# A written order for three engines in the expert stage of a transformer block

## The chip, the cores and the metric

The kernel runs on one core of a Trainium2 chip. Five engines work side by side, each through its own list of instructions, in order: TensorE (PE, matmuls), VectorE (DVE), ScalarE (ACT), GpSimd (POOL) and SyncE (SP, which issues transfers); the DMA engines move the data. The metric is the time of one execution on the device in microseconds; the lower the better.

## The reference, cut to what matters

One block over 512 tokens of width 1024: a mixer of two kinds of attention, then a sparse expert layer. Only the expert layer is touched.

```python
logits = (hf @ router_w + router_b).astype(jnp.float32)
top_val, top_idx = lax.top_k(logits, TOP_K)          # 4 of 32 experts per token
gate = jax.nn.softmax(top_val, axis=-1)
...
def expert_block(args):                              # up to 128 tokens of one expert
    e, toks, wts = args
    u = hf[toks] @ w1[e] + b1[e]                     # 1024 -> 2048
    g_, lin = u[:, :D_FF], u[:, D_FF:]
    g_ = jnp.minimum(g_, SWIGLU_LIMIT)
    lin = jnp.clip(lin, -SWIGLU_LIMIT, SWIGLU_LIMIT)
    y = ((lin + 1.0) * g_ * jax.nn.sigmoid(SWIGLU_ALPHA * g_)) @ w2[e] + b2[e]   # 1024 -> 1024
    return y * wts[:, None]
...
out = jax.ops.segment_sum(y.reshape(R, D), row_tok, num_segments=T)
```

All weights are float32: 12 MiB per expert, 384 MiB for the 32.

## The kernel before, in words

The attention half runs first. The router's tail then writes the normalised rows to a table in DRAM (`h2d`) and computes, for each token and expert, the token's place among that expert's 128 slots (`pos_e`). The expert stage follows, one expert after another, a slot without a token being given token 0 and gate 0. An expert with more than 128 tokens is finished in a loop at the end, of which no instruction appears in the profile.

**Precision.** Each product of float32 values is made of three matmuls: both operands are split into a high part (rounded to a matmul's input type) and a low part (the rest), and high x high, high x low and low x high are summed in PSUM (`mm3`, L85 to L88, one matmul per line L86 to L88).

**Weights.** An expert has 12 chunks of 128x2048, 1 MiB each: eight of `w1`, four of `w2`. The list `order` (L949 to L954) runs through the eight chunks of expert e, then the four `w2` chunks of expert e-1. `ready(i)` (L965) does two things: it asks for loads up to seven chunks ahead (`LOAD_AHEAD`, L33; there are seven raw buffers, L57 and `rawx`), which SP issues at L64 once a buffer is free, and it splits chunks i and i+1 with `split2` (L668): a cast on ACT at L673 (`whi`) and a subtraction on DVE at L674 (`wlo`), into eight buffers, so four chunks.

**Token rows.** `prep(e)` (L919) has four parts, which are called for the next expert at several places of the current one: `slots` compares `pos_e` with the slot numbers (`oh`, L928), `infos` looks up token and gate by a small matmul (`pi`, L934), writes the indices (`idx`, L936) and gathers the rows by an indirect DMA from POOL (`xg`, L909), and `turn(h)` transposes half of the rows on PE (`pxt`, L916) and makes from it the high part (ACT, L943) and the low part (DVE, L944) of `XT`, which is the stationary operand of the first layer.

**One expert.** Four bias matmuls start the four PSUM banks `pu` (L990). For each of the eight `w1` chunks twelve matmuls of 512 columns follow, three for each bank. `act_half` (L882) makes silu (`sg`, ACT, L886), clamp and product (`lc`, DVE, L887 and L889). The products are transposed during the next expert's chunks 1 and 2 (`pat`, L895) and split (`ahi` L1008, `alo` L1009), and the four `w2` chunks give `py`, twelve matmuls each. `emit` (L898) scales `py` into `ys` (DVE, L901) and adds the rows to the output by an indirect DMA (L903). `add_b2` (L702) adds the second bias for 128 tokens in each of four experts.

**Order.** The program is written in this sequence, but the order in which each engine gets its instructions is set by a scheduler at build time, which goes by priorities (the sequence of writing) and its own estimate of when operands are ready. So a weight cast of a later chunk may stand ahead of the cast of `XT`. Within an engine nothing overtakes.

## Time and profile before

| | |
|---|---|
| three runs, us | 1645.16, 1646.41, 1641.27 (median 1645.16) |
| the profiled execution, us | 1644.42 |
| its span, first to last instruction, us | 1642.6 |
| mean granted TensorE clock over the span | 0.985 |
| busy over the span | PE 94%, DVE 82%, ACT 61%, POOL 19% |
| bytes by DMA | 492.97 MB, of them 449.56 by SP's queue (weights) and 35.66 by POOL's |

The expert stage fills the span from about 383 us, the first bias matmul, to the end. A row of a timeline has the start, the duration, engine, line, operation, output <- inputs, and in brackets the engine's idle time before it with what ended it. A row of waits has the waiting engine, tile and line, what ended the wait, the sum in us, how often and the longest. A row of groups has the count, after it the summed busy time, the mean in ns and the idle time before.

### The profile page before, as it was taken

The page shows a single profiled execution, that of the slowest core. Times are in us where ns is not written, and L with a number is a line of the kernel's source. Part 1 is how long each engine was busy: PE and PEld are TensorE (multiplying, and loading weights), DVE is VectorE, ACT ScalarE, POOL GpSimd, SP SyncE. Part 2 cuts the span into 40 slices and gives each one's busy share as a digit, 9 for nine tenths or more (in the row PEclk, how much of TensorE's full clock was granted, in tenths as well). Part 3 has the DMA queues.
Part 4 walks back from the last instruction along what each step waited for, and adds up shares of the span by engine and source line. Part 5 has one row for each costly group of instructions (what it writes and reads, how often), then busy time and mean ns, then how long its engine had stood idle before and what let it go on. Part 6 is the DMA issues. An engine that isn't in the chain of part 4 may idle for free. (4 is left out here: it accounts for less than half of the span.)

```text
span 1642.6 us, 20317 instructions
## 1 busy us (share of the span) xinstructions
PE 1542.9 (94%) x7541; PEld 1216.0 (74%) x7541; DVE 1351.8 (82%) x1578; ACT 1005.9 (61%) x1023; POOL 309.0 (19%) x259
## 2 busy tenths in 40 slices
PE   7998999997999999999999999999999999999996
PEld 6886644575777777787787878787878777878785
DVE  4879488556888888898888989898989898889885
ACT  4333376633667766666666766666666676666663
POOL 2217255311122011111101010211111111010110
PEclk9999999997999999999999999999999999999998
DMA  9754132066899999999999999999999999999992
GB/s 342 253 199 109 52 103 78 1 209 255 307 358 357 368 363 369 351 357 363 355 348 352 369 354 368 350 365 348 359 356 368 357 352 360 341 366 360 350 363 69
DMA packets 113405, 492.97 MB, mean 300 GB/s; under 512 B 9936, under 2 KB 22288, under 8 KB 80536
## 3 DMA queue, kind: packets, MB, share of 16 engines
q1 hardware_dynamic: 100600, 449.56, 73.0%
q0 software_dynamic: 9792, 35.66, 8.8%
q10 hardware_dynamic: 2912, 6.44, 1.1%
q8 instruction: 60, 0.98, 0.2%
q14 instruction: 41, 0.34, 0.1%
HBM read 468.55 MB, written 23.07 MB: 299 GB/s over the span
## 5 line engine op out<-in xcount | busy, mean ns | idle before, releaser
L674 DVE TENSOR_TENSOR wlo<-w,whi 128x2048 fp32r<-128x2048 f32 x384 | 870.8, 2287 | 128.8 <-ACT whi L673 118.4
L673 ACT CAST whi<-w 128x2048 fp32r<-128x2048 f32 x384 | 729.2, 1907 | 345.9 <-PE pu L87 247.5
L86 PE MATMUL pu<-whi,XT 128*128 128x512 f32 x1024 | 412.4, 404 | 28.7 <-ACT XT L943 28.7
L88 PE MATMUL pu<-whi,XT 128*128 128x512 f32 x1024 | 389.2, 395 | 18.8 <-DVE XT L944 18.8
L87 PE MATMUL pu<-wlo,XT 128*128 128x512 f32 x1024 | 405.1, 396 | 0.0
L86 PEld LDWEIGHTS pu<-whi,XT 128*128 128x128 f32 x1024 | 193.6, 189 | 75.7 <-ACT XT L943 36.4
L88 PEld LDWEIGHTS pu<-whi,XT 128*128 128x128 f32 x1024 | 191.6, 188 | 67.5 <-DVE XT L944 26.6
L87 PEld LDWEIGHTS pu<-wlo,XT 128*128 128x128 f32 x1024 | 193.9, 189 | 37.9
L88 PE MATMUL py<-whi,alo 128*128 128x512 f32 x512 | 201.2, 393 | 0.0
L87 PE MATMUL py<-wlo,ahi 128*128 128x512 f32 x512 | 200.9, 392 | 0.0
L909 POOL DMA_INDIRECT xg<-h2d,idx x32 | 84.4, 2638 | 526.5 <-issue 439.0
L86 PE MATMUL py<-whi,ahi 128*128 128x512 f32 x512 | 181.4, 393 | 0.3 <-DVE ys L901 0.3
L903 POOL DMA_INDIRECT out_dram<-ys,idx x32 | 79.5, 2485 | 497.4 <-DVE ys L901 497.4
L86 PEld LDWEIGHTS py<-whi,ahi 128*128 128x128 f32 x512 | 96.2, 188 | 21.7 <-issue 0.7
L87 PEld LDWEIGHTS py<-wlo,ahi 128*128 128x128 f32 x512 | 96.2, 188 | 21.6
L88 PEld LDWEIGHTS py<-whi,alo 128*128 128x128 f32 x512 | 96.2, 188 | 21.4
L86 PE MATMUL pz<-whi,hhi 128*128 128x512 f32 (+2 forms) x224 | 81.4, 366 | 5.0 <-ACT hsq L391 3.6
L87 PE MATMUL pz<-wlo,hhi 128*128 128x512 f32 (+2 forms) x224 | 78.7, 354 | 0.0
L88 PE MATMUL pz<-whi,hlo 128*128 128x512 f32 (+2 forms) x224 | 77.4, 355 | 0.0
L196 ACT ACTIVATE pr<-sb,sm 128x256 f32<-128x256 f32 (+3 forms) x93 | 51.7, 557 | 20.8 <-DVE sm L193 17.7
L157 DVE SCALAR_TENSOR_TENSOR am<-ada,cond,am 128x256 f32<-128x256 f32 x128 | 59.7, 502 | 0.8 <-DMA ada<-in_ada_w_dram 0.5
L943 ACT CAST XT<-pxt 128x512 fp32r<-128x512 f32 x64 | 34.6, 586 | 32.8 <-PE pxt L916 32.8
(292 smaller groups left out, 1671.5 us busy)
## 6 DMA issues: line engine op xcount, KB each, us to landing
w<-in_exp_w_dram SPq DMA_DIRECT2D x384, 1024.0 KB, 7.4
ada<-in_ada_w_dram SPq DMA_DIRECT2D x22, 1024.0 KB, 6.4
win<-in_w_in_dram SPq DMA_DIRECT2D x6, 1024.0 KB, 5.0
win<-in_w_in_dram SPq DMA_DIRECT2D x3, 768.0 KB
x<-in_x_dram SPq DMA_DIRECT2D x4, 512.0 KB
ada<-in_ada_w_dram SPq DMA_DIRECT2D x4, 512.0 KB, 4.7
wo<-in_w_out_dram SPq DMA_DIRECT2D x4, 512.0 KB, 6.5
wo<-in_w_out_dram SPq DMA_DIRECT2D x2, 1024.0 KB
```

The costliest lines, as they stand in the source:

```text
L86: T.matmul(o, lhi, rhi, start=start, stop=False, **kw)
L87: T.matmul(o, lhi, rlo, start=False, stop=False, **kw)
L88: T.matmul(o, llo, rhi, start=False, stop=stop, **kw)
L157: V.scalar_tensor_tensor(am[:, p:p + MOD_W], rr[k // 4][:, c0:c0 + MOD_W], cond[:, k:k + 1], am[:, p:p + MOD_W], op0=ALU.mult, op1=ALU.add)
L196: A.activation(tl[i], sb[:, :n], AF.Exp, scale=-1.0, bias=sm[:, 0, i:i + 1], accum_out=sm[:, 1, i:i + 1])
L673: A.copy(hi, r)
L674: V.tensor_sub(lo, r, hi.bitcast(F32))
L903: G.indirect_dma_start(out=out_rows, out_offset=bass.IndirectOffsetOnAxis(ap=icol, axis=0), in_=ys, in_offset=None, compute_op=ALU.add, bo ...
L909: G.indirect_dma_start(out=xg, out_offset=None, in_=h2d, in_offset=bass.IndirectOffsetOnAxis(ap=icol, axis=0), bounds_check=S - 1, oob_is_ ...
L943: A.copy(XT[:, 0, hs], pt)
```

## The change

**A step** is now one chunk of weights, so 12 per expert. In the order of writing, a step i asks for the loads, does what PE has to do beside the products (`pes`), the products of chunk i, the cast of chunk i+3 on ACT (`high`), what ACT has to do beside (`acts`), what DVE has to do beside (`dves`), and the subtraction of chunk i+3 on DVE (`low`).

**The order is fixed.** `in_order` goes through all instructions of PE, DVE and ACT from the first step on and ties each to the one before it on its engine, so that the scheduler keeps the written order. POOL and SP are not tied.

**Rows two experts ahead.** During expert e the slots of expert e+2 are compared at step 4, looked up at step 7, and its indices are written and its rows gathered at step 9, into one of two fixed buffers. The rows of expert e+1 are transposed at steps 4 and 5 and split at steps 4 to 6. For the first two experts this is done ahead of the first step.

**The products** of a chunk come as four matmuls high x high, four high x low part of the rows, four low part of the weights x high, over the four banks in turn, instead of three for one bank after the other.

**Slots without tokens** get an index above 511 (`none`), and gather and scatter leave out rows whose index is out of bounds. The two row buffers are filled with zeros once.

The rest: the silu, clamp and product are called at steps 8 and 9; `add_b2` is in two parts, at steps 9 and 11, with an output buffer of its own; `info` and `idx` have four buffers instead of three.

The core of the diff:

```diff
+SPLIT_AHEAD = 3
-B2_AT = 6
+    def in_order(start):
+        last = {}
+        for ins in traced()[start:]:
+            if ins.engine in (T.engine, V.engine, A.engine):
+                if ins.engine in last:
+                    tc.add_manual_dep(ins, last[ins.engine].name,
+                                      mybir.DependencyInfo(mybir.DependencyClass.NoSync, mybir.DependencyReason.DATA),
+                                      reason="order of issue")
+                last[ins.engine] = ins
...
+        V.tensor_scalar(none, cnt, piota, float(S), op0=ALU.is_le, op1=ALU.mult)
...
-                             in_=ys, in_offset=None, compute_op=ALU.add, bounds_check=S - 1, oob_is_err=True)
+                             in_=ys, in_offset=None, compute_op=ALU.add, bounds_check=S - 1, oob_is_err=False)
...
+    xgs = [ep.tile([P, D], F32, tag=f"xg{q}", name="xg", bufs=1) for q in range(2)]
+    for xg in xgs:
+        G.memset(xg, 0.0)
...
-            V.tensor_copy(info, pi)
-            V.tensor_copy(idx, info[:, 0:1])
+        def fetch():
+            V.tensor_copy(info, g["pi"])
+            V.tensor_add(idx, info[:, 0:1], none[:, e:e + 1])
+            gather(idx, xgs[e % 2])
             V.tensor_add(info[:, 3:4], info[:, 1:2], info[:, 2:3])
-            g[0] = gather(idx, xp)
...
-        for a in range(i, min(i + 2, len(order))):
-            if a in raws:
-                chunks[a] = split2(raws.pop(a))
+    def step(i, pe=(), products=(), act=(), dve=()):
+        load(i + SPLIT_AHEAD)
+        for f in pe:
+            f()
+        hi, lo = chunks.pop(i)
+        for f in products:
+            f(hi, lo)
+        more = i + SPLIT_AHEAD < len(order)
+        if more:
+            high(i + SPLIT_AHEAD)
+        for f in act:
+            f()
+        for f in dve:
+            f()
+        if more:
+            low(i + SPLIT_AHEAD)
...
+        if two_on:
+            dves[4].append(two_on.slots)
+            pes[7].append(two_on.lookup)
+            dves[9].append(two_on.fetch)
+        if one_on:
+            for h in range(2):
+                pes[4 + h].append(lambda h=h, p=one_on: p.turn(h))
+                acts[4 + h].append(lambda h=h, p=one_on: p.high(h))
+                dves[5 + h].append(lambda h=h, p=one_on: p.low(h))
...
-                for g in range(2):
-                    for h in range(2):
-                        cs = slice(1024 * g + 512 * h, 1024 * g + 512 * h + 512)
-                        mm3(pu[h][g], XT[:, 0, c, :], XT[:, 1, c, :], hi[:, cs], lo[:, cs], False, c == KD - 1)
+                def first(hi, lo, c=c):
+                    for w, x, last in ((hi, 0, False), (hi, 1, False), (lo, 0, c == KD - 1)):
+                        for h in range(2):
+                            for g in range(2):
+                                c0 = 1024 * g + 512 * h
+                                T.matmul(pu[h][g], XT[:, x, c, :], w[:, c0:c0 + 512], start=False, stop=last)
+                step(i, pes[c], [first], acts[c], dves[c])
...
     late.pop()()
+    in_order(start)
```

Where it moves instructions. First PE, at the border between the last `w2` chunk of one expert and the first `w1` chunk of the next, before (`pxt` are the transposes of the rows):

```order
L86 MATMUL py<-whi,ahi 128x512
L87 MATMUL py<-wlo,ahi 128x512
L88 MATMUL py<-whi,alo 128x512
L916 MATMUL pxt<-ident,xg 128x128 x8
L86 MATMUL pu<-whi,XT 128x512
L87 MATMUL pu<-wlo,XT 128x512
```

With the change, the same border, and then the place in the middle of the eight `w1` chunks to which the transposes have gone:

```order
L1145 MATMUL py<-whi,ahi 128x512 x4
L1145 MATMUL py<-whi,alo 128x512 x4
L1145 MATMUL py<-wlo,ahi 128x512 x4
L1106 MATMUL pu<-biasr,bsel 128x512 x4
L1121 MATMUL pu<-whi,XT 128x512 x8
```

```order
L1121 MATMUL pu<-wlo,XT 128x512 x4
L949 MATMUL pxt<-ident,xg 128x128 x4
L1121 MATMUL pu<-whi,XT 128x512 x8
L1121 MATMUL pu<-wlo,XT 128x512 x4
L949 MATMUL pxt<-ident,xg 128x128 x4
```

The eight transposes no longer stand directly ahead of the matmuls that read their result, but, in two groups, some eight steps ahead of them.

Second DVE, from the scaling of an expert's output (`ys`) to the first half of the next `alo`, before, for the expert whose timeline the prediction shows:

```order
L901 SCALAR_TENSOR_TENSOR ys<-py,info,g2row 128x512 x2
L674 TENSOR_TENSOR wlo<-w_8782,whi 128x2048
L674 TENSOR_TENSOR wlo<-w_8800,whi 128x2048
L944 TENSOR_TENSOR XT<-pxt,XT 128x512 x2
L674 TENSOR_TENSOR wlo<-w_8825,whi 128x2048
L674 TENSOR_TENSOR wlo<-w_8850,whi 128x2048
L1009 SCALAR_TENSOR_TENSOR alo<-pat,ahi 128x512
```

With the change, steps 0 to 6 of an expert:

```order
L931 SCALAR_TENSOR_TENSOR ys<-py,info,g2row 128x512 x2
L1019 TENSOR_TENSOR wlo<-w_8468,whi 128x2048
L1019 TENSOR_TENSOR wlo<-w_8487,whi 128x2048
L1078 SCALAR_TENSOR_TENSOR alo<-pat,ahi 128x512
L1019 TENSOR_TENSOR wlo<-w_8512,whi 128x2048
L1078 SCALAR_TENSOR_TENSOR alo<-pat,ahi 128x512
L1019 TENSOR_TENSOR wlo<-w_8534,whi 128x2048
L961 TENSOR_TENSOR oh<-siota,pos_e 128x512
L1019 TENSOR_TENSOR wlo<-w_8560,whi 128x2048
L983 TENSOR_TENSOR XT<-pxt,XT 128x512
L1019 TENSOR_TENSOR wlo<-w_8578,whi 128x2048
L983 TENSOR_TENSOR XT<-pxt,XT 128x512
```

Each subtraction of a weight chunk (`wlo`, L1019) now has at most two other instructions between it and the next, and the low half of `XT` is that of the expert to come. ACT, before and with the change, at the cast of `XT`:

```order
L673 CAST whi<-w_8782 128x2048
L673 CAST whi<-w_8800 128x2048
L943 CAST XT<-pxt 128x512 x2
L673 CAST whi<-w_8825 128x2048
L673 CAST whi<-w_8850 128x2048
L1008 ACTIVATE ahi<-pat 128x512
```

```order
L1074 ACTIVATE ahi<-pat 128x512
L1015 CAST whi<-w_8534 128x2048
L1015 CAST whi<-w_8560 128x2048
L979 CAST XT<-pxt 128x512
L1015 CAST whi<-w_8578 128x2048
L979 CAST XT<-pxt 128x512
L1015 CAST whi<-w_8612 128x2048
```

The two casts of `XT` stand one step apart, each behind one weight cast, and after the casts of `ahi` rather than before them.

More of the change, by code (lines that the diff above doesn't have):

```diff
@@ L1 @@
 import itertools
+from types import SimpleNamespace
 from contextlib import ExitStack
@@ L968, in ready, with high, low @@
                 raws[a] = load_raw(w_src(*order[a]), f"w{a}")
-        for a in range(i, min(i + 2, len(order))):
-            if a in raws:
-                chunks[a] = split2(raws.pop(a))
-    turn_in, cur = prep(0)
-    ready(0)
-    for f in turn_in:
-        f()
-    pos_i = 0
+    def high(i):
+        hi = next(wq_pools).tile([P, 2048], F32R, tag="wq", name="whi")
+        lo = next(wq_pools).tile([P, 2048], F32R, tag="wq", name="wlo")
+        chunks[i] = hi, lo
+        A.copy(hi, raws[i])
+    def low(i):
+        hi, lo = chunks[i]
+        V.tensor_sub(lo, raws.pop(i), hi.bitcast(F32))
+    def step(i, pe=(), products=(), act=(), dve=()):
[14 more added lines that the diff above has]
+            low(i + SPLIT_AHEAD)
+    load(0)
+    for i in range(SPLIT_AHEAD):
+        high(i)
+        low(i)
+    preps = {e: prep(e) for e in range(2)}
+    for e in range(2):
+        preps[e].slots()
+        preps[e].lookup()
+        preps[e].fetch()
+    for h in range(2):
+        preps[0].turn(h)
+        preps[0].high(h)
+        preps[0].low(h)
+    start = len(traced())
+    i = 0
     prev = None
@@ L980, in block_kernel, with turned, high_a, low_a @@
     for e in range(NE + 1):
-        nxt = None
-        if e + 1 < NE:
-            steps, nxt = prep(e + 1)
+        two_on = preps[e + 2] if e + 2 in preps else None
+        if e + 2 < NE:
+            two_on = preps[e + 2] = prep(e + 2)
+        one_on = preps.get(e + 1)
+        pes = [[] for _ in range(12)]
+        acts = [[] for _ in range(12)]
+        dves = [[] for _ in range(12)]
+        if prev:
+            for h in range(2):
+                def turned(h=h, p=prev):
+                    p.pt[h] = act_T(p.lc[h])
+                def high_a(h=h, p=prev):
+                    ahi = ep.tile([P, 4, P], F32R, tag=f"ahi{h}", name="ahi", bufs=1)
+                    alo = ep.tile([P, 4, P], F32R, tag=f"alo{h}", name="alo", bufs=1)
+                    p.a[h] = ahi, alo
+                    A.activation(ahi, p.pt[h], AF.Copy, scale=1.0 / ALPHA)
+                def low_a(h=h, p=prev):
+                    ahi, alo = p.a[h]
+                    V.scalar_tensor_tensor(alo, p.pt[h], 1.0 / ALPHA, ahi.bitcast(F32), op0=ALU.mult, op1=ALU.subtract)
+                pes[1 + h].append(turned)
+                acts[1 + h].append(high_a)
+                dves[2 + h].append(low_a)
+        if late:
+            dves[0].append(late.pop())
+        if two_on:
[3 more added lines that the diff above has]
+        if one_on:
+            for h in range(2):
+                pes[4 + h].append(lambda h=h, p=one_on: p.turn(h))
+                acts[4 + h].append(lambda h=h, p=one_on: p.high(h))
+                dves[5 + h].append(lambda h=h, p=one_on: p.low(h))
+        if 1 <= e <= NT:
+            gates, add = add_b2(e - 1, ep)
+            pes[9].append(gates)
+            pes[11].append(add)
+        this = None
         if e < NE:
-            XT, info, idx = cur
+            me = preps.pop(e)
+            XT = me.XT
             sel = [bsel[:, v, e:e + 1].to_broadcast([P, P]) for v in range(2)]
@@ L1015, in block_kernel @@
-            this = ([act_half(pu[h], ep) for h in range(2)], [], info, idx)
-        else:
-            for h in range(2):
-                pt = act_T(prev[0][h])
-                ahi = ep.tile([P, 4, P], F32R, tag=f"ahi{h}", name="ahi", bufs=1)
-                alo = ep.tile([P, 4, P], F32R, tag=f"alo{h}", name="alo", bufs=1)
-                A.activation(ahi, pt, AF.Copy, scale=1.0 / ALPHA)
-                V.scalar_tensor_tensor(alo, pt, 1.0 / ALPHA, ahi.bitcast(F32), op0=ALU.mult, op1=ALU.subtract)
-                prev[1].append((ahi, alo))
-            late.pop()()
+            halves = [act_half(pu[h], ep) for h in range(2)]
@@ L1094, in block_kernel @@
         XT = ov.tile([P, KD, P], F32, name="XTo")
-        xg = gather(idx, ov)
+        xg = ov.tile([P, D], F32, name="xgo")
+        G.memset(xg, 0.0)
+        gather(idx, xg)
         for h in range(2):
```

148 lines of the change are left out of this document (78 added, 70 removed).

## The prediction

> **What bounds the kernel now.** I read the page's first part, then the table of stretches, then who waited for whom on TensorE, then the timeline of the engines named there. The change touches the expert stage alone, so the page serves for the base of the sum only:
>
> ```profile
> span 1642.6 us, 20317 instructions
> PE 1542.9 (94%) x7541; PEld 1216.0 (74%) x7541; DVE 1351.8 (82%) x1578; ACT 1005.9 (61%) x1023; POOL 309.0 (19%) x259
> ```
>
> In the profiled execution, which took 1644.42 us (1.8 us around its span; the median of the three runs shown is 1645.16, 0.7 us more), PE is the fullest engine. The timeline (start, duration, engine, line) has the bias matmuls of expert 3 and, 28 periods on, of expert 31:
>
> ```profile
> 504.52 0.85 PE L990 MATMUL pu<-biasr,bsel 128*128 128x512 f32 x3
> 1576.96 1.09 PE L990 MATMUL pu<-biasr,bsel 128*128 128x512 f32 x4
> ```
>
> That is (1576.96 - 504.52) / 28 = 38.30 us an expert. The table of stretches gives the length, the busy time of PE, PE's weight loads, DVE, ACT and POOL, the granted clock, the DMA share and GB/s:
>
> ```profile
> 505.00:1577.00 1072.00, 1027.61 (x4710) 836.52 (x4709) 951.38 (x730) 720.96 (x513) 149.42 (x59) 1.00 0.98 358
> 1013.00:1017.00 4.00, 4.00 (x23) 3.27 (x22) 3.35 (x2) 2.68 (x3) 0.00 (x0) 1.00 1.05 274
> 1018.00:1027.00 9.00, 9.00 (x43) 7.43 (x42) 8.38 (x8) 6.04 (x5) 0.00 (x0) 1.00 1.03 421
> 1033.00:1038.00 5.00, 5.00 (x23) 4.08 (x22) 5.00 (x5) 4.11 (x3) 0.00 (x0) 1.00 0.85 318
> ```
>
> Over the first PE is busy 96%, DVE 89% (951.38 / 1072, so 34.0 us an expert), ACT 67%, the clock is 1.00, and the DMA engines show a share of 0.98 at 358 GB/s. Two resources look full. What PE really waits for stands in its list of waits for 500 to 1600 us, which holds experts 3 to 31, 29 of them:
>
> ```profile
> PE pu L86 <- ACT XT L943: 26.1, 29, 1.4
> PE pu L88 <- DVE XT L944: 18.5, 17, 1.5
> ```
>
> Nothing else is on it: no weight chunk, no transfer. PE waits only for XT, the transposed token rows, once an expert for the high part and in 17 of 29 for the low part. The timeline around expert 17 shows why:
>
> ```profile
> 1013.55 0.60 PE L895 MATMUL pat<-ident,lc 128*128 128x128 f32 x4
> 1013.91 0.48 PE L86 MATMUL pu<-whi,XT 128*128 128x512 f32 x1
> ...
> 1043.57 1.03 PE L916 MATMUL pxt<-ident,xg 128*128 128x128 f32 x8
> 1045.97 0.50 PE L86 MATMUL pu<-whi,XT 128*128 128x512 f32 x1 [1.37 <-ACT XT L943]
> 1047.69 0.40 PE L87 MATMUL pu<-wlo,XT 128*128 128x512 f32 x1
> 1049.58 1.20 PE L88 MATMUL pu<-whi,XT 128*128 128x512 f32 x4 [1.49 <-DVE XT L944]
> ...
> 1043.54 1.90 ACT L673 CAST whi<-w 128x2048 fp32r<-128x2048 f32 x1 [0.84 <-PE py L87]
> 1045.34 1.07 ACT L943 CAST XT<-pxt 128x512 fp32r<-128x512 f32 x2
> ...
> 1044.44 4.48 DVE L674 TENSOR_TENSOR wlo<-w,whi 128x2048 fp32r<-128x2048 f32 x2
> 1048.84 1.28 DVE L944 TENSOR_TENSOR XT<-pxt,XT 128x512 fp32r<-128x512 f32 x2
> ```
>
> The eight transposes of the rows stand directly ahead of the matmuls that need them. ACT starts a 1.90 us weight cast just before they end, and the XT cast queues behind it; DVE has 4.48 us of weight splits ahead of the low part. Neither engine is short of time; XT is last in both queues.
>
> **The change part by part.** *XT is turned an expert early (steps 4 and 5 of the expert before).* This removes both waits. The listed idle time is less than the loss, since the modelled busy time of a matmul overlaps its successor. Undisturbed, the 512-column matmuls start 0.23 us apart, as the four in the row at 1049.58 do ((1.20 - 0.39 for the last, less 0.11 for the first after a wait) / 3). A transpose takes (1.03 - 0.60) / 4 = 0.11, so the last of the eight starts at 1044.33, and the next matmul 1.64 later, where after the four `pat` transposes it started 0.03 later (1013.91 against 1013.55 + 3 x 0.11). Lost: 1.61 for 1.37 listed, 0.24 more. For the low part 1049.58 - 1047.69 - 0.23 = 1.66 for 1.49 listed, 0.17 more. Experts 3 to 31: 26.1 + 29 x 0.24 + 18.5 + 17 x 0.17 = 54.4 us. The same list for 428 to 500 us has 2.6 and 0.3 us for experts 1 and 2:
>
> ```profile
> PE pu L86 <- ACT XT L943: 2.6, 2, 1.4
> PE pu L88 <- DVE XT L944: 0.3, 1, 0.3
> ```
>
> Expert 2's part is about half of the first and all of the second, with the additions 1.3 + 0.24 + 0.3 + 0.17 = 2.0 us. Expert 1 is a case of its own, below. Sum: 56.4 us.
>
> *What hides the moved work.* The transposes, casts and subtractions of XT are as many as before, in two groups of four rather than one of eight; that splits nothing that costs. Rows must be there by step 4: the indices are now written at step 9 of the expert two before, seven steps or about 21 us ahead. The gather's group and its time to landing:
>
> ```profile
> L909 POOL DMA_INDIRECT xg<-h2d,idx x28 | 74.9, 2674 | 461.2 <-issue 409.6 <-PE pu L87 17.6 <-PE pu L88 14.0
> ...
> DMA to landing us min/median/max: 7.7/9.9/11.3
> ```
>
> 2.7 on POOL and up to 11.3 to land make 14.0, so 7 us are spare.
>
> *The new order of the matmuls* (hi x XThi, hi x XTlo, lo x XThi, four each) keeps their number and size. The run of four at 1049.58 is already in that form, one stationary tile on four banks, and runs at 0.23. Cost nothing; a dearer stream is bounded by nothing in the trace that is slower.
>
> *Splits three chunks ahead.* Number and size stay. A step is 12 matmuls, 2.76 us. The cast of chunk i+3 may start when the matmuls on the high part of chunk i-1 are done, two thirds through that step; 1.9 (cast) and 2.29 (subtraction) later it is ready, some 3.3 us into step i, and it is needed 8.3 us after that step's start. DVE's heaviest stretch, steps 8 and 9, holds two clamps, two products, three small ones and two splits, about 7.7 us where PE spends 5.5; the 2.2 us that it falls behind fit in the 5 spare. Cost nothing; the other bound is a rival.
>
> *Loads.* Seven buffers still hold the raw chunks, and the queue waits for a buffer, not for the DMA (rows of SP's waits, of the DMA issues with the time to landing last, and of the queues):
>
> ```profile
> SPq L64 <- DVE wlo L674: 931.4, 332, 8.6
> w<-in_exp_w_dram SPq DMA_DIRECT2D x384, 1024.0 KB, 7.4
> q0 software_dynamic: 9792, 35.66, 8.8%
> ```
>
> At 36.4 us an expert a buffer turns in 7 x 36.4 / 12 = 21.2 us; less 7.4 to land and 4.2 for cast and subtraction, 9.6 are spare. Rate: with no gather or scatter the engines move 421 GB/s (1018 to 1027), so an expert's 12 chunks, 12.58 MB, need 29.9 us. In 1013 to 1017, with a scatter, the 1.10 MB moved hold 0.52 MB of it; the rest is worth 1.4 us, so a scatter costs 2.6; a gather likewise (1033 to 1038) at most 2.5. Together 35.0 us, under 36.4 even if nothing is skipped. The share of 0.98 is occupancy, not a limit reached.
>
> *Empty slots skipped.* 512 tokens with four experts each fill 2048 of the 4096 slots. Queue q0 carries 35.66 MB, 2.1 of them the four bias sums, so half of 33.6 goes, 0.52 MB an expert. As the DMA does not bind, I take nothing for it; the last scatter, which nothing hides, may land up to 2 us earlier.
>
> *Expert 1.* Expert 0 has no second-layer chunks behind it, so expert 1's bias matmuls wait for expert 0's clamps.
>
> ```profile
> 426.84 0.40 PE L88 MATMUL pu<-whi,XT 128*128 128x512 f32 x1
> 427.08 1.03 PE L916 MATMUL pxt<-ident,xg 128*128 128x128 f32 x8
> 428.16 1.52 PE L990 MATMUL pu<-biasr,bsel 128*128 128x512 f32 x3
> 430.92 0.79 PE L86 MATMUL pu<-whi,XT 128*128 128x512 f32 x1 [1.24 <-ACT XT L943]
> ...
> 428.44 1.28 DVE L887 TENSOR_SCALAR lc<-pu 128x512 f32<-128x512 f32 x2
> ```
>
> From 427.07 to 430.92 there are 0.87 of transposes and 0.69 of bias matmuls: 2.3 us lost. With XT made earlier, the last clamp ends some 1.7 us after the products (the previous split leaves DVE 0.3 late), of which 0.7 are bias matmuls: 1.0 lost. Gain 1.3.
>
> *Losses.* At the end, the `pat` transposes of expert 31 now follow the last chunk of expert 30 instead of standing among its matmuls; PE then waits for cast and scaled outputs 0.8 instead of 0.4 us. At the front two fills of the row buffers (128x1024) enter POOL's queue between two steps of the router's tail, ahead of a step that PE's slot lookup awaits:
>
> ```profile
> 356.47 2.41 POOL L792 TENSOR_TENSOR xt<-xt,sh2row 128x1024 f32<-128x1024 f32 x1 [2.56 <-DVE xt L791]
> 390.20 0.29 POOL L706 COPY g<-gatef 128x128 f32<-128x128 f32 x1 [2.70 <-DVE m L795]
> ```
>
> Each costs at most the 2.41 of a two-input operation of that size, and 2.70 idle us take most of both: between 0 and 2.1, I take 1.0.
>
> Sum: 56.4 + 1.3 - 0.4 - 1.0 = 56.3, and 1644.4 - 56.3 = 1588 us. An expert then takes 38.30 - 54.4 / 28.5 = 36.4 us.
>
> **The rivals.** *The transfers bind at the rate they show now.* If 358 GB/s is what the chip gives over a whole expert, 421 being a short burst, the bytes set the pace: 358 x 38.30 = 13.71 MB now, 13.19 without the empty slots, 36.8 us: 0.4 us above 36.4, 31 experts, 1588 + 14 = 1602; with nothing skipped 1644. For it: the share of 0.98. Against it: 9 us on end at 421, and no wait for a chunk. The Trainium skill has that figure as a rule: "DMA: Bandwidth & Descriptors", section "Bandwidth", puts about 358 GB/s as the limit of HBM for one core, and says that for loads from HBM this side binds. The row of 421 GB/s disagrees for this core running alone. 12%.
>
> *The fixed order hands DVE's waits to PE.* From 500 to 1600 us DVE idles for the casts:
>
> ```profile
> DVE wlo L674 <- ACT whi L673: 97.8, 153, 2.1
> ```
>
> That is 97.8 / 28.7 = 3.4 us an expert. If each split still meets its cast late in the written order, DVE needs 34.0 + 3.4 = 37.4, 1.0 more than PE: 31 x 1.0 on 1588 = 1619. Against it: three chunks of lead. 10%.
>
> *The stall only moves.* PE, no longer held at XT, meets another operand at once and keeps 38.3 an expert: 1644, give or take 5. Against it: both other engines have over 2 us idle per expert. 5%.
>
> *Slower: the rows come late.* Transposes of step 4 that wait for a gather stop PE, and with the order fixed everything behind stops too; formerly only the next expert waited. It decides from 21 us between index and landing; each us beyond costs 31 us, so from 23 us the kernel is slower than before. Skipped slots would have to cost POOL some 10 us a gather, against 2.7 for a whole one; at 24 us, 1588 + 93 = 1681. 4%.
>
> That the skip removes no packet (a fifth to a quarter likely) leaves the time at 1588, since 35.0 us still fit.
>
> **How the numbers follow.** Forecast 1588 with 69%, from 1580 (the last scatter 2 us shorter, no loss at the front, up to 0.15 us an expert more from the small gaps behind transposes) to 1598 (0.3 us an expert left). The range for 8 in 10 reaches over the first rival and the second: 1580 to 1620. About 5 us, 0.3%, can be told from no change: faster 69 + 12 + 10 = 91%, within 5% (the stall that moves), slower 4%.
>
> **What would show it.** Right: PE's list of waits has no XT row in the stage; the bias matmuls stand 36.4 us apart; q0 falls to about 19 MB; PE over 99% busy. First rival: casts that wait for the landing of `w`, the buffer queue no longer on DVE. Second: matmuls on `wlo` waiting for DVE. Last: `pxt` waiting for `xg`. Wrong altogether: an interval above 38 us with XT early.

## The result, and the profile after

| | before | changed |
|---|---|---|
| runs, us | 1645.16, 1646.41, 1641.27, 1642.66 (median 1643.91) | 1579.75, 1571.62, 1577.07, 1576.09 (median 1576.58) |
| ratio, 95% interval | | 0.9588 (0.9558 to 0.9618) |
| profiled execution, span, us | 1644.42, 1642.6 | 1579.75, 1577.9 |

The forecast was 1588 us with a range from 1580 to 1620; the kernel is 3.4 us faster than the low end. The page after, parts 1, 3 and 5 (busy time and its share; a queue's packets, MB and share; a group's count, busy time, mean ns and the idle time before it):

```profile
span 1577.9 us, 20293 instructions
PE 1522.1 (96%) x7541; PEld 1214.0 (77%) x7541; DVE 1352.7 (86%) x1579; ACT 1007.1 (64%) x1023; POOL 294.2 (19%) x261
...
q0 software_dynamic: 9792, 18.90, 5.3%
...
L942 POOL DMA_INDIRECT xg<-h2d,idx x32 | 46.1, 1440 | 649.9 <-PE py L1145 591.8
```

PE has as many matmuls as before, and VectorE and ScalarE are busy as long (1351.8 and 1005.9 us before), in a shorter span. The skip takes the bytes of the empty slots away, 35.66 to 18.90 MB, with as many packets as before. The waits from 500 to 1600 us (the whole list of PE, then DVE's row for the casts):

```profile
PE py L1145 <- DVE ys L931: 0.9, 1, 0.9
...
DVE wlo L1019 <- ACT whi L1015: 59.5, 167, 1.6
```

The first row is all that is left on PE's list, and it belongs to the last expert: both XT rows are gone, and nothing took their place. DVE still waits for casts (59.5 us, 97.8 before), but PE never waits for DVE's splits. The table of stretches has PE busy throughout the stage (columns as in the prediction):

```profile
505.00:1515.00 1010.00, 1010.00 (x4712) 835.39 (x4711) 952.00 (x727) 724.16 (x514) 135.67 (x59) 1.00 0.98 366
```

The timeline, with the bias matmuls of experts 3 and 31 and two groups of four second-layer matmuls between them:

```profile
506.33 1.09 PE L1106 MATMUL pu<-biasr,bsel 128*128 128x512 f32 x4
...
1037.71 1.07 PE L1145 MATMUL py<-whi,alo 128*128 128x512 f32 x4
1038.62 1.07 PE L1145 MATMUL py<-wlo,ahi 128*128 128x512 f32 x4
...
1515.24 1.09 PE L1106 MATMUL pu<-biasr,bsel 128*128 128x512 f32 x4
```

(1515.24 - 506.33) / 28 = 36.03 us an expert, against 38.30 before and 36.4 forecast. The two groups say where the other 0.37 us may come from: (1038.62 - 1037.71) / 4 = 0.2275, within the rounding of the rows, and over all py matmuls from 616 to 1500 us the mean from start to start is 0.2267 us. Before the change it was 0.230 in both layers (worked out from the trace in the same way, consecutive matmuls of one layer, gaps over 0.3 us left out). No row of the list shows a wait in these gaps; the same matmuls simply follow one another faster.

Bias matmul to bias matmul, the 64.7 us between the two profiled executions divide as follows: expert 0 loses 4.1 (49.02 us to expert 1's bias matmuls, 44.89 before), expert 1 is level (37.44 and 37.34), expert 2 gains 2.4 (36.65 and 39.02), the 28 periods from expert 3 to 31 gain 63.5, and from there to the end it is 3.0 less (62.7 and 65.7).

So two things had to be found: what shortened the gap between matmuls, and what made the first expert late.

### The profile page after: what moved, and what is told of

Its sections match the earlier page's. It is cut to its first block, busy times and chain, and to the rows that moved or that the text cites. A ratio compares the mean times of both kernels' runs of the same rounds, so it can differ in the third digit from the quotient of the medians.

```text
span 1577.9 us, 20293 instructions
## 1 busy us (share of the span) xinstructions
PE 1522.1 (96%) x7541; PEld 1214.0 (77%) x7541; DVE 1352.7 (86%) x1579; ACT 1007.1 (64%) x1023; POOL 294.2 (19%) x261
## 3 DMA queue, kind: packets, MB, share of 16 engines
q0 software_dynamic: 9792, 18.90, 5.3%
## 4 chain that ended last, share of the span: by engine, by line
PE 83%; DMA 5%; issue 4%; DVE 4%; POOL 1%; ACT 1%; SPq 0%; POOLq 0%; DVEq 0%; ACTq 0%
PE pu L1121 42%; PE py L1145 20%; PE po L637 2%; DMA out_dram<-ys,idx 2%; PE pxt L949 2%; PE pz L87 2%; PE pu L1106 2%; PE pz L88 2%; PE pz L89 2%; PE pat L925 2%; PE pp L616 1%; PE ps L204 1%; DMA ada<-in_ada_w_dram 1%; DVE am L172 1%; PE pw L88 1%
## 5 line engine op out<-in xcount | busy, mean ns | idle before, releaser
L1019 DVE TENSOR_TENSOR wlo<-w,whi 128x2048 fp32r<-128x2048 f32 x384 | 873.5, 2288 | 72.4 <-ACT whi L1015 71.8
L1121 PE MATMUL pu<-whi,XT 128*128 128x512 f32 x2048 | 526.2, 399 | 0.0
L1121 PE MATMUL pu<-wlo,XT 128*128 128x512 f32 x1024 | 275.0, 390 | 0.0
L942 POOL DMA_INDIRECT xg<-h2d,idx x32 | 46.1, 1440 | 649.9 <-PE py L1145 591.8
L933 POOL DMA_INDIRECT out_dram<-ys,idx x32 | 102.6, 3207 | 295.5 <-DVE ys L931 255.8
L1145 PE MATMUL py<-whi,ahi 128*128 128x512 f32 x508 | 136.6, 390 | 1.0 <-DVE ys L931 0.9
L1145 PE MATMUL py<-whi,alo 128*128 128x512 f32 x508 | 135.8, 389 | 0.0
L1145 PE MATMUL py<-wlo,ahi 128*128 128x512 f32 x508 | 135.8, 389 | 0.0
L88 PE MATMUL pz<-wlo,hhi 128*128 128x512 f32 (+2 forms) x224 | 78.7, 354 | 0.0
L81 ACT CAST whi<-win 128x1024 fp32r<-128x1024 f32 (+3 forms) x28 | 24.2, 871 | 46.1 <-PE pz L88 21.3
L87 PEld LDWEIGHTS pz<-whi,hhi 128*128 128x128 f32 x224 | 42.4, 190 | 14.4 <-ACT hsq L406 5.6
L208 DVE CUSTOM_DVE_ANT_0 sb<-ps,dtile 128x128 f32<-128x128 f32 (+3 forms) x96 | 43.9, 482 | 9.4 <-PE ps L204 6.5
```

Source lines behind the costliest of these rows:

```text
L87: T.matmul(o, lhi, rhi, start=start, stop=False, **kw)
L88: T.matmul(o, lhi, rlo, start=False, stop=False, **kw)
L208: V.tensor_tensor_reduce(sb[:, :n], p[:, :n], dtile[:, 384 - P * i:512], scale=-0.125 * 2.0 ** -(h + 1), scalar=-NEG, op0=ALU.add, op1=ALU ...
L933: G.indirect_dma_start(out=out_rows, out_offset=bass.IndirectOffsetOnAxis(ap=icol, axis=0), in_=ys, in_offset=None, compute_op=ALU.add, bo ...
L942: G.indirect_dma_start(out=xg, out_offset=None, in_=h2d, in_offset=bass.IndirectOffsetOnAxis(ap=icol, axis=0), bounds_check=S - 1, oob_is_ ...
L1019: V.tensor_sub(lo, raws.pop(i), hi.bitcast(F32))
```

## The experiments

### Is it the order of the matmuls?

The change gives PE the same matmuls in another order, so that was the first theory. The changed kernel with the old order (`mm3` is that of L85 to L88 before):

```diff
-                    for w, x, last in ((hi, 0, False), (hi, 1, False), (lo, 0, c == KD - 1)):
+                    for g in range(2):
                         for h in range(2):
-                            for g in range(2):
-                                c0 = 1024 * g + 512 * h
-                                T.matmul(pu[h][g], XT[:, x, c, :], w[:, c0:c0 + 512], start=False, stop=last)
+                            cs = slice(1024 * g + 512 * h, 1024 * g + 512 * h + 512)
+                            mm3(pu[h][g], XT[:, 0, c, :], XT[:, 1, c, :], hi[:, cs], lo[:, cs], False, c == KD - 1)
```

and so for `py`.

> The changed kernel with one thing put back: each accumulator again takes its three products one after the other (high x high, high x low part of the weights, low x high), as before the change. Theory, the order of the matmuls sets their spacing: it goes from 0.227 back to 0.230 us, 148 matmuls x 31 experts x 0.0030 = some 12 us, so 1588 us. Rival, the spacing fell because something else eased (empty slots no longer moved, no stops at XT): the spacing stays at 0.227 and the time at 1577.

Measured 1578.94 us (ratio 0.9606, 0.9585 to 0.9628), an expert 36.03 us (here and below the mean of the 28 periods from expert 3 to 31), py at 0.2267. Neither moved, and the theory falls with its 12 us. The next kernel put five orders into one execution, four experts each (`orders(e, cells)` gives a list of accumulator, stationary part, moving part; in `Hw`, `Lw` and `Hl` the capital letter stands for the high or low part of the rows, the small one, w or l, for the high or low part of the weights):

```diff
+        Hw, Lw, Hl = (0, 0), (1, 0), (0, 1)
+        if 9 <= e < 13:
+            return [(b, *p) for b in cells for p in (Hw, Hl, Lw)]
+        if 13 <= e < 17:
+            a = [(b, *((Hw, Lw)[q % 2])) for q, b in enumerate(cells)]
+            return a + [(b, *((Lw, Hw)[q % 2])) for q, b in enumerate(cells)] + [(b, *Hl) for b in cells]
+        if 17 <= e < 21:
+            return [(b, *p) for b in cells for p in (Hw, Hl)] + [(b, *Lw) for b in cells]
+        if 21 <= e < 25:
+            return [(b, *p) for b in cells for p in (Hw, Lw)] + [(b, *Hl) for b in cells]
+        return [(b, *p) for p in (Hw, Lw, Hl) for b in cells]
...
```

> The changed kernel with a different order of the same matmuls in groups of four experts. Experts 5 to 8 and from 25 on: the new order (control, 36.0 us). 9 to 12: the old one (36.4 if the order is the cause). 13 to 16: the accumulators still take turns and the weight tile is still used in runs, but the stationary tile changes at every matmul of the first two thirds: 36.4 if changing the stationary tile costs, 36.0 if not. 17 to 20: two products in a row into one accumulator on one stationary tile, the moving tile in turn whi and wlo: 36.4 if writing one accumulator twice running costs (or changing the moving tile), 36.0 if only the stationary tile counts. 21 to 24: two products in a row into one accumulator with the same moving columns, stationary tile changed: 36.4 if the accumulator or the stationary tile counts, 36.0 if the moving tile is the cause.

From expert 8 to expert 30 all periods, whatever the order, lie between 35.99 and 36.03 us, and the execution took 1573.36. Neither the accumulator, nor the change of the stationary tile, nor that of the moving tile between matmuls counts. The counterpart, the kernel before with the new order alone:

> The kernel before, with only the new order of the matmuls (high x high on all accumulators, then low part of the rows, then low part of the weights); XT still turned just ahead of its use, every slot gathered and scattered. Theory of the order: spacing 0.227 us, 12 us gained, 1633 us, with the XT waits of 1.4 to 1.5 us an expert still in place. Rival (something else eased the spacing): 1644, spacing 0.230.

Measured 1676.38 us (1.0218, 1.0196 to 1.0239), slower, which neither expected. PE's waits from 500 to 1600 us, and the stretch:

```profile
PE pu L999 <- DVE XT L944: 39.4, 25, 2.0
PE pxt L916 <- DMA xg<-h2d,idx: 8.1, 1, 8.1
PE pu L999 <- ACT XT L943: 5.0, 21, 0.2
```

```profile
505.00:1515.00 1010.00, 961.26 (x4327) 779.39 (x4326) 870.99 (x671) 665.25 (x471) 157.24 (x55) 0.98 0.97 349
```

The scheduler, still free, shifted its order with the products: the wait for XT's high part has nearly gone and that for its low part has doubled, but their sum, 44.4 us, is that of the kernel before (44.6). New are one gather that came 8.1 us late, and the granted clock: 0.98 over this stretch, where the kernel before had 1.00. In the trace it stands at half in nine places, 37.5 us in all, which costs matmuls up to 18.8 us. An expert takes 39.23 us, 26 us more over the 28 periods; the late gather and the clock cover that. Why the clock fell is not shown. The time therefore says nothing on the question; the spacing, counted outside the slow places, does: 0.2304 in pu, 0.2313 in py, no faster than before.

### Is it the traffic of the empty slots?

`fetch` without the skip, so that empty slots gather row 0 and add zeros to it again:

```diff
-            V.tensor_add(idx, info[:, 0:1], none[:, e:e + 1])
+            V.tensor_copy(idx, info[:, 0:1])
```

> The changed kernel without the skipping of empty slots: they gather row 0 and add zeros to it, as before the change. Theory (place of the tiles; the DMA does not bind): spacing 0.2267 us and an expert 36.0 us as with skipping, the last scatter up to 2 us later, 1577 to 1579 us. Rival (traffic of the empty rows disturbs the matmuls): 0.230 us and 36.4 us an expert, 1588. First rival of the prediction (358 GB/s bind): 38.3 us an expert, 1645.

Measured 1578.2 us (0.9604, 0.9580 to 0.9627), 36.03 us an expert, py at 0.2267. Its queue row and its stretch:

```profile
q0 software_dynamic: 9792, 35.66, 9.0%
```

```profile
505.00:1515.00 1010.00, 1010.00 (x4713) 835.40 (x4712) 951.45 (x728) 724.95 (x514) 132.46 (x59) 1.00 1.00 381
```

With all bytes moved the core takes 381 GB/s at the same pace. The skip is worth nothing that can be measured, and the 358 GB/s of the kernel before were not a limit.

### Is it where the tiles lie?

One edit had not been looked at: `info` and `idx` got one buffer more each. In the built program each such buffer takes 32 bytes of a partition, so everything allocated behind them, `XT`, `ahi` and `alo` (the stationary tiles of the two layers) among it, moved by 64 bytes against the weight tiles `whi` and `wlo` (the moving tiles). The traces hold no addresses; places and distances below are those of the built programs, and between two runs they differ by the unused tiles that the runs add. An unused tile undoes that, or does it to the kernel before:

```diff
+        xp.tile([P, 16], F32, tag="pad", name="pad", bufs=1)
         XT = xp.tile([P, 2, KD, P], F32R, tag="XT", name="XT")
```

In the changed kernel:

> The changed kernel with one unused tile of 64 bytes a partition ahead of XT, so that XT, ahi and alo (the stationary tiles) start at 32 modulo 128 bytes, as in the kernel before; the change had moved them to 96 modulo 128, because it gave info and idx four buffers instead of three. Nothing else is changed. Theory, the place of the stationary tiles sets the spacing of the matmuls: 0.230 us again, an expert 36.4 instead of 36.0 us, 1588 us. Rival, the spacing fell since the rest of the core is quieter (half of the rows not moved, no stops): 36.0 and 1577.

In the kernel before:

> The kernel before with the same unused 64 bytes ahead of XT, which here moves XT, ahi and alo from 32 to 96 modulo 128 bytes. Theory of the place: undisturbed matmuls 0.2267 us apart, 148 matmuls x 31 experts x 0.003 = up to 13 us less, 1631 us, the XT waits as before. Rival (quieter core): 0.230 us apart and 1643.

Measured 1599.37 us (0.9745, 0.9729 to 0.9761) and 1634.6 us (0.9964, 0.9952 to 0.9975): 64 bytes that nobody reads cost the changed kernel 23 us, and in the kernel before they gain 7 (1641.33 in the same session), with XT waits as before (26.1 and 19.0 us). The place is the cause; but 1599 is beyond what the old spacing explains, and what about the place counts was still open. Three more runs:

> The changed kernel with 64 unused bytes ahead of XT and 64 more behind it, ahead of the pool that holds ahi, alo, lc and ys: XT starts at 32 modulo 128 bytes, all others at 96 as in the change. Theory, the place of the stationary tile itself sets the spacing: the matmuls of pu go to 0.233 us, those of py stay at 0.2267; an expert about 36.5 us (two thirds of the 0.71 us that moving both costs), 1592 us. Rival, it is one of the other tiles that moved with them (lc, ys, ahi): pu stays as it is, 36.0 and 1577.

> The changed kernel with 32 unused bytes ahead of XT and 64 more ahead of ahi and alo: XT at 0 modulo 128 bytes, ahi and alo at 64. If 96 alone is good, pu and py both run at 0.229 to 0.233 us and an expert takes 36.4 to 36.7 us; if 32 alone is bad, both stay at 0.2267 and 36.0; if the two differ, pu shows what 0 does and py what 64 does.

> The changed kernel with the split weights whi and wlo (the moving tiles) shifted by 64 bytes to 32 modulo 128, and XT, ahi and alo held at 96. If the place of the stationary tile counts by itself: 0.2267 us and 36.0 us an expert, 1577. If what counts is that stationary and moving tile lie alike modulo 128 bytes (both at 96 in the change, 32 and 96 before): 0.230 to 0.233 and 36.4 to 36.7, 1590 to 1599.

They took 1599.2, 1602.84 and 1601.21 us, and the first theory of the place falls: with XT alone at 32 modulo 128 the matmuls of py became slow too, though ahi lay at 96 as in the fast kernel; and shifting only the moving tiles is as bad. What fits all is the distance between stationary and moving tile modulo 256 bytes, 0 in every fast kernel. In the run that moved XT alone, ahi had ended up 128 from the weights. Three more, to break that if it is wrong:

> The changed kernel with 64 unused bytes ahead of XT and 192 more ahead of ahi and alo: XT lies 64 modulo 256 bytes from the weight tiles, ahi and alo 0. Theory, the distance between stationary and moving tile modulo 256 decides, for each pair by itself: the matmuls of pu at 0.233 us, those of py at 0.2267 once undisturbed; an expert 36.4 to 36.5 us, some 1591. Rival, any shift of XT slows all that follows, as where XT alone seemed to be moved: both at 0.232 to 0.233 and 36.7.

> The changed kernel with 256 unused bytes ahead of XT: all distances to the weight tiles stay the same modulo 256, and change modulo 512 (from 256 to 0). Theory: 0.2267 us, 36.0 us an expert, 1572 to 1580. If the period is 512 bytes, or if an added tile in itself slows the matmuls: 36.4 to 36.8.

> The changed kernel with 64 unused bytes ahead of the weight tiles, so that moving and stationary tiles shift together (160 modulo 256 bytes in place of 96). Theory of the distance: 0.2267 us and 36.0 us an expert, 1572 to 1580. If the place by itself counts: 36.4 to 36.8 and 1588 to 1602.

1590.19, 1575.19 and 1575.95 us: as the distance says, each layer by itself. The timeline of the first, with two rows of a step of the first layer (XT at distance 64) and two groups of the second (ahi and alo at 0):

```profile
1035.38 2.03 PE L1123 MATMUL pu<-whi,XT 128*128 128x512 f32 x8
1037.25 1.09 PE L1123 MATMUL pu<-wlo,XT 128*128 128x512 f32 x4
...
1043.27 1.07 PE L1147 MATMUL py<-wlo,ahi 128*128 128x512 f32 x4
1044.17 1.07 PE L1147 MATMUL py<-whi,ahi 128*128 128x512 f32 x4
```

(1037.25 - 1035.38) / 8 = 0.234 and (1044.17 - 1043.27) / 4 = 0.225. Last, the change at the distance that the kernel before has, 192, and the two values left:

> The changed kernel with 192 unused bytes ahead of XT, so that XT, ahi and alo lie 192 modulo 256 bytes from the weight tiles, as in the kernel before. Theory, the distance is the whole miss: undisturbed matmuls 0.229 to 0.230 us apart, 36.4 us an expert, 1588 to 1592 us (the first expert stays 4 us late). Rival, every distance but 0 costs what 64 does: 0.233, 36.7, 1599.

> The changed kernel with XT at 160 and ahi and alo at 224 modulo 256 bytes from the weight tiles. If only 0 is free of the loss, pu and py both stay above 0.229 us: 36.3 to 36.8 us an expert, 1586 to 1603. If one of the two is as good as 0, its matmuls stand 0.2267 us apart.

1587.55 us (0.9667, 0.9651 to 0.9683) and 1593.89 us. Of the first, bias matmuls of experts 3 and 31, and two groups of py:

```profile
504.15 1.08 PE L1107 MATMUL pu<-biasr,bsel 128*128 128x512 f32 x4
...
1040.43 1.10 PE L1146 MATMUL py<-whi,alo 128*128 128x512 f32 x4
1041.36 1.10 PE L1146 MATMUL py<-wlo,ahi 128*128 128x512 f32 x4
...
1522.93 1.08 PE L1107 MATMUL pu<-biasr,bsel 128*128 128x512 f32 x4
```

(1522.93 - 504.15) / 28 = 36.39 us an expert, (1041.36 - 1040.43) / 4 = 0.2325, again within the rounding. All kernels of the series (mean spacing from start to start, 616 to 1500 us, in ns; the means of pu hold some ten unsteady gaps after each group of transposes, so 229 is the best that pu shows):

| distance of XT; of ahi, alo | kernel | pu, ns | py, ns | an expert, us | time, us |
|---|---|---|---|---|---|
| 0; 0 | changed | 229.1 | 226.7 | 36.03 | 1576.58 |
| 0; 0 | changed, XT 256 further on | 229.1 | 226.7 | 36.03 | 1575.19 |
| 0; 0 | changed, all 64 further on | 228.7 | 226.7 | 36.00 | 1575.95 |
| 0; 0 | before, padded | 228.9 | 226.9 | 38.08 | 1634.6 |
| 32; 96 | changed | 233.2 | 234.4 | 36.80 | 1602.84 |
| 64; 64 | changed | 233.0 | 233.3 | 36.75 | 1599.37 |
| 64; 64 | changed, weights moved | 233.0 | 233.3 | 36.74 | 1601.21 |
| 64; 128 | changed | 233.2 | 232.5 | 36.68 | 1599.2 |
| 64; 0 | changed | 233.3 | 227.3 | 36.47 | 1590.19 |
| 160; 224 | changed | 233.0 | 233.4 | 36.72 | 1593.89 |
| 192; 192 | changed | 229.6 | 233.3 | 36.39 | 1587.55 |
| 192; 192 | before | 229.9 | 230.0 | 38.30 | 1643.91 |

Why the distance counts is not shown by these runs; that it counts, and with which period, is. (The weight tiles were moved only together with their neighbours, so that they and no neighbour are the partner is argued, from their being the moving operand.) The 192 rows are not settled entirely either: py runs at 233 in the changed kernel and at 230 before. The traces show two steady patterns of gaps at this distance, 226, 229, 232 ns and 233, 233, 234; in the changed kernel py keeps to the second throughout, in the kernel before to the first for some three quarters of its gaps. What selects one is open.

The Trainium skill, "SBUF — State Buffer", section "Who interferes with whom", has one rule for conflicts on the memory: only the port pair that VectorE and GpSimd share causes contention. That rule does not account for the table, in which TensorE loses up to 3% by where its own two operands lie; whether this is contention is not known.

### Which part of the change emptied PE's waits?

The lead of three chunks, cut to two (`SPLIT_AHEAD = 2`):

> The changed kernel with the splits two chunks ahead instead of three, the order still fixed. As the prediction has it, three chunks of lead cost nothing; whether they bring something is open. If VectorE's lag behind the casts is what they cover: waits for wlo around steps 8 and 9, up to 1.0 us an expert, 1600 to 1610. If two chunks would do: 36.0 us an expert and 1572 to 1580.

Measured 1574.1 us (0.9580, 0.9560 to 0.9600), 36.03 us an expert: two would do. Next, the order left to the scheduler again (the call of `in_order` taken out), with everything else of the change, distance 0 included:

> The changed kernel without the fixed order: the planner again chooses the order on TensorE, VectorE and ScalarE, with the code, the three chunks of lead, the early XT and the skipped slots unchanged. Its order puts the bias matmuls of an expert among its first products and the slot lookup later. Theory (an early XT and rows on time are what pays): no XT wait, 36.0 to 36.4 us an expert, 1577 to 1588. Rival (the written order is what pays): waits of 1 to 2 us an expert come back at other places, 1610 to 1645.

Measured 1603.61 us (0.9766, 0.9739 to 0.9792), 36.9 us an expert from expert 8 on. The waits of PE from 500 to 1600 us, and the timeline at an expert's end:

```profile
PE pu L1106 <- DVE lc L913: 7.9, 24, 0.3
PE py L1145 <- DVE wlo L1019: 2.1, 3, 1.3
...
```

```profile
936.68 1.07 PE L1121 MATMUL pu<-wlo,XT 128*128 128x512 f32 x4
938.08 0.49 PE L1106 MATMUL pu<-biasr,bsel 128*128 128x512 f32 x1 [0.33 <-DVE lc L913]
```

XT is on time, but now the bias matmuls of the next expert stand directly behind the last products, ahead of the second layer, and wait for the clamp to free their bank: 938.08 - 936.68 - 4 x 0.227 = 0.49 us lost. That is about half of the 0.9; the rest is spread over smaller gaps. And the reverse, order fixed, but XT made at the border as before:

```diff
-        if one_on:
+        if 1 <= e < NE:
             for h in range(2):
-                pes[4 + h].append(lambda h=h, p=one_on: p.turn(h))
-                acts[4 + h].append(lambda h=h, p=one_on: p.high(h))
-                dves[5 + h].append(lambda h=h, p=one_on: p.low(h))
+                pes[0].append(lambda h=h, p=preps[e]: p.turn(h))
+            for h in range(2):
+                pes[0].append(lambda h=h, p=preps[e]: p.high(h))
+                pes[0].append(lambda h=h, p=preps[e]: p.low(h))
```

> The changed kernel, order still fixed and all else as in the change, but XT is made from the gathered rows right ahead of the first products of its own expert, behind the bias matmuls, as before the change (its cast now stands ahead of the next weight cast, its subtraction behind the splits already queued). Theory, the early XT is worth what the prediction gave it: 1.0 to 2.6 us an expert come back as waits for XT, 1607 to 1657 us. Rival, three chunks of lead and the fixed order would have emptied the queues ahead of XT anyway: at most 0.6 us an expert, 1577 to 1595.

Measured 1591.73 us (0.9685, 0.9662 to 0.9708), 36.48 us an expert, 0.45 more than the change: the rival holds. PE's waits, and ScalarE at the border of an expert:

```profile
PE pu L1122 <- ACT XT L979: 6.9, 29, 0.2
```

```profile
1019.85 1.07 ACT L979 CAST XT<-pxt 128x512 fp32r<-128x512 f32 x2 [3.08 <-PE pxt L949]
```

In the written order ScalarE has been idle for 3.08 us when the transposes end, where before the change it had just begun a cast of 1.90. At distance 0 there are thus four corners: 1634.6 with neither (the padded kernel before), 1603.6 with XT early but no written order, 1591.7 with the written order but XT late, 1576.6 with both. The second and the third are each one edit away from the last, so that 15 us for the early XT and 27 for the written order, each with the other in place, are clean. The first differs from the others in the rest of the change too. Of that, the skip, the third chunk and the order of the products are worth nothing by the runs above, but those runs had the order written out (with the scheduler free, the new order of the products made the kernel before slower, 1676.38 us), and the rest, such as the fetch two experts ahead, was not tried by itself. If it is worth little, the two overlap: 31 and 43 us alone, 58 together.

### What makes the first expert late?

The front of the kernel before, POOL and PE:

```profile
395.76 1.31 POOL L909 DMA_INDIRECT xg<-h2d,idx  x1 [5.09 <-DVE info L937]
...
400.69 1.94 PE L916 MATMUL pxt<-ident,xg 128*128 128x128 f32 x8 [6.58 <-DMA xg<-h2d,idx]
402.45 0.79 PE L86 MATMUL pu<-whi,XT 128*128 128x512 f32 x1
```

and of the changed one, POOL, DVE and PE:

```profile
390.11 1.87 POOL L938 MEMSET xg<- 128x1024 f32 x2 [2.66 <-DVE aux L833]
397.36 3.06 POOL L942 DMA_INDIRECT xg<-h2d,idx  x1 [4.96 <-DVE info L973]
...
396.96 2.29 DVE L1019 TENSOR_TENSOR wlo<-w,whi 128x2048 fp32r<-128x2048 f32 x1 [0.44 <-issue]
...
405.26 1.97 PE L949 MATMUL pxt<-ident,xg 128*128 128x128 f32 x8 [7.75 <-DMA xg<-h2d,idx]
407.05 3.71 PE L1121 MATMUL pu<-whi,XT 128*128 128x512 f32 x8
```

In the changed kernel the gather starts 1.60 us later, behind the fill. The gather then lasts 1.75 longer: a split has begun on VectorE 0.40 ahead of it, and the gather ends at 400.42, 1.17 after that split (399.25), about the 1.31 that it takes alone. (The Trainium skill, "SBUF — State Buffer", section "SBUF: two separate sides", says that a VectorE operation with two inputs in SBUF holds the port pair that the two engines share against a GpSimd operation that reads SBUF, and that the one that starts later waits for the whole instruction. The subtraction has two such inputs, and the gather takes its indices from SBUF; these rows agree. A gather further on, which began 0.03 us after a split and was not held up, does not.) The rows land another 1.2 later, which the rows do not explain. Together the first product is 4.60 us late. Expert 0 takes 4.1 longer and not 4.6, since the granted clock, which is reduced there in both kernels, was 0.65 over the five microseconds from the first product on, and 0.55 before the change. Without the fill, the first two experts gathering all rows so that the buffers hold numbers:

```diff
-    for xg in xgs:
-        G.memset(xg, 0.0)
...
+            if e < 2:
+                V.tensor_copy(idx, info[:, 0:1])
+            else:
+                V.tensor_add(idx, info[:, 0:1], none[:, e:e + 1])
```

> The changed kernel without the two fills of the row buffers; the first two experts gather all 128 rows instead (empty slots take row 0 with weight zero, as before the change), so the buffers hold numbers from then on. Theory, the first expert is 4.6 us later than before since the fill (1.87 us on GpSimd) stands ahead of what the slot lookup waits for and the gather then runs beside VectorE's splits: the fill's share is 1.5 to 2 us, so 1575 us; the rest, a gather of 3.1 instead of 1.3 us, stays. Rival, the fill delays everything that is late there: the first matmul of the stage comes back to 402.5 us and the time falls to 1572. If the fill is not on the path: 1577.

```profile
395.44 1.29 POOL L940 DMA_INDIRECT xg<-h2d,idx  x1 [5.08 <-DVE info L974]
...
396.67 4.49 DVE L1020 TENSOR_TENSOR wlo<-w,whi 128x2048 fp32r<-128x2048 f32 x2 [0.54 <-ACT whi L1016]
...
400.17 1.97 PE L947 MATMUL pxt<-ident,xg 128*128 128x128 f32 x8 [4.50 <-DMA xg<-h2d,idx]
401.96 2.81 PE L1122 MATMUL pu<-whi,XT 128*128 128x512 f32 x8
```

Measured 1572.86 us (0.9580, 0.9564 to 0.9596; 1572.13 to 1573.82): the rival of that expectation holds, the gather is all but past when the split begins (396.73 and 396.67), and everything late there comes back; bias matmul to bias matmul, expert 0 takes 43.24 us, 5.8 less than in the changed kernel. The first product accounts for 4.8 of that (19.0 us after the first bias matmul, and 23.8 in the changed kernel), the granted clock for the other 1.0: it was 0.85 over five microseconds from the first product on. Against the changed kernel's 1576.58 the intervals overlap, but its four runs lie within 1.7 us where those of the change lie within 8. In the execution with the five orders, whose front is that of the change, the gather and a split began within 0.03 us of each other, the gather took 1.29, and expert 0 45.5; so it was at distances 160 and 224, where the gather began 0.66 ahead of the split (1.29 and 45.4). A race of some tenths of a microsecond may thus be part of what spreads the runs of the change. The granted clock goes with the spread too, 0.988 over the fastest run and 0.985 over the slowest; which brings which is not shown.

## Why the prediction was right, and where it was wrong

**XT waits, 56.4 us.** Right as to how they show, and near in size: at the distance of the kernel before the change takes 36.39 us an expert, where 36.4 was forecast, and 1587.55 us, where 1588 was. That it agrees so closely is in part luck. py runs at 233.3 ns there and ran at 230.0 before, 48 x 3.3 ns = 0.16 us an expert that the forecast did not have. At distance 0, with the same spacing before and after, an expert gains 38.08 - 36.03 = 2.05 us, where 1.9 was forecast. And the time holds some 4 us that the first expert loses. Not right in what brings the gain: the early XT was given all of it, but with the order written out a late XT costs only 15 us, and an early XT without the written order leaves 27 of the gain out. The reading of the profile (neither engine short of time, XT last in both queues) was the better guide than the edit that the gain was booked on.

**The new order of the matmuls, "cost nothing".** This is the step that failed, in the half that says the run of four "runs at 0.23". The order indeed costs nothing. But 0.23 was taken as a property of the matmul, and it is one of where its operands lie. The buffers added for `info` and `idx`, which the sum has no term for, moved the stationary tiles to distance 0: 36.39 - 36.03 = 0.36 us an expert, 11.2 us over 31, 11.0 from the medians of the two runs (1587.55 and 1576.58). Measured in the kernel before, the same move is worth less, 38.30 - 38.08 = 0.22 us an expert or 6.8 over 31, since py ran at 230 there. With either amount put back, the time lies between 1583 and 1588, inside the range.

**The balance.** Between the two profiled executions 56.3 us were forecast and 64.7 measured. The 28 periods gave 11.0 more (63.5, and 28 x 54.4 / 29 = 52.5), expert 2 0.4 more, the end 1.5 more, experts 0 and 1 4.5 less. The median of the changed kernel lies another 3.2 us below its profiled execution.

**The front, a loss of 1.0.** Mis-sized: with expert 1's share (a gain of 1.3 forecast) experts 0 and 1 were to gain 0.3 and lost 4.2. The bounds priced the fill's own time on POOL, and not what a later gather runs into: of the 4.60 us, 1.60 are the later start, 1.75 the longer gather, and 1.2 the later landing, which stays open.

**The end, a loss of 0.4.** Together with expert 31's own XT wait, 1.9, a gain of 1.5 was forecast and 3.0 measured; the last scatter is no shorter (12.1 us from the end of its instruction to the end of the span, 12.0 before), so skipped slots gain nothing there.

**Splits three ahead, loads, skipped slots: nothing.** Right: two chunks of lead take the same time, and with every slot moved neither the time nor PE's waits change.

**The rivals.** 358 GB/s as a limit: refuted by 381 GB/s at 36.03 us an expert with every slot moved. The Trainium skill, "DMA: Bandwidth & Descriptors", section "Bandwidth", gives about 358 GB/s also as what each core gets when both cores of a memory domain stream; as a limit it does not show here, with one core running. DVE's waits handed to PE: 59.5 us of them stay, 2.1 an expert, and PE sees none. The moved stall and the late rows: no such row on PE's list.

## What to carry to other kernels

A change of a buffer's size or number can move what is allocated behind it; before a difference of one or two per cent is credited to an edit, look whether the spacing of undisturbed matmuls changed, and compare at the same distance between stationary and moving tile. A wait for a small operand at the end of long queues can be cured by making it earlier or by ordering the queues; price them together, since their gains overlap. An instruction added to an idle engine costs what it makes late, and what that then collides with.

## What the runs showed of the hardware that was not expected

The gap between 512-column matmuls depends on the distance of the two operands' addresses within a partition modulo 256 bytes: in the second layer 226.7 to 227.3 ns at 0, in both layers more at each of the other multiples of 32 that they were given (32, 64, 160 and 192 for XT; 64, 96, 128, 192 and 224 for ahi and alo: up to 234.4); 256 more bytes change nothing, nor, at 0, does the order of the matmuls. At 0 the gaps after an interruption need some ten matmuls to settle (224 to 236 ns) and then stay at 226 or 227; at the other distances repeating patterns stay, such as 226, 229, 232 or 233, 233, 234, and both of these occur at 192. An indirect gather whose instruction starts on GpSimd 0.4 us after a 2.29 us subtraction has begun on VectorE ended 1.2 us after that subtraction; one that started 0.03 us after it, or before, took 1.3 us. Rows with an index out of bounds take their bytes from the queue's account, but not their packets.
